# A hybrid attention and RWKV-7 layer on one core: transposing transfers sent piece by piece, and weight transfers issued three tiles ahead

## The chip, the core and the metric

The kernel runs on one core of a Trainium2 chip. Its engines run side by side and wait for each other through semaphores: TensorE (PE, matmuls and their weight loads PEld), VectorE (DVE), ScalarE (ACT), GpSimd (POOL) and SyncE (SP), which here does nothing but issue DMA transfers. Each engine takes its instructions in the order in which the built program holds them, SP its transfers too. The metric is the device time of one execution in microseconds (us), the median over runs.

## The reference

One layer over 256 tokens of width 4096. One projection of the input (4096 x 18640 columns) feeds 16 heads of forgetting attention ("fox"), 32 heads of RWKV-7 time mixing and a gate path; an output projection (4096 x 4096) and a LayerNorm with residual follow.

```python
proj = jnp.einsum('bsd,dc->bsc', x, w_in)
fox_out = _fox_attention(fq, fk, fv, log_sigmoid(ff + f_bias))   # causal softmax with decay, 16 heads of 128
rw = rw + (rw_prev - rw) * mu_shift                              # shift by one token, then r, k, v, decay, a
kk = kk / jnp.maximum(jnp.linalg.norm(kk, axis=-1, keepdims=True), 1e-12)
y = _rwkv7_scan(rh, decay, kh, vh, -kk, kk * ah)
# S_t = S_{t-1} diag(decay_t) + (S_{t-1} a_t) b_t^T + v_t k_t^T ;  y_t = S_t r_t, 32 heads of 64
y = groupnorm(y) * gn_gain + gn_bias + jnp.sum(rh * kh * r_k, axis=-1, keepdims=True) * vh
h = jnp.concatenate([fox_out, y], axis=-1) * jax.nn.silu(z)
x = layernorm(ALPHA * x + jnp.einsum('bsc,cd->bsd', h, w_out))
```

## The kernel before, in words

**The stream of weight tiles.** The input projection is cut into 8 groups n of 4 blocks b (two blocks of recurrent columns, b = 0 for r and k and b = 1 for the values, then b = 2 and 3, each with the queries, keys and gates of one pair of heads); the output projection into 8 blocks. A block has 16 weight tiles of 128 x 1024 float32 (512 KB), called `w<n>_<b>_<q>` or `wo<b>_<q>`. Every tile is loaded by SP (L217), rounded to fp32r on ACT (the high part `h`, L140) and subtracted on DVE (the low part `l`, L141, "the split"); then PE does 12 matmuls of 512 columns with it, four times the three products x_high·w_high, x_low·w_high, x_high·w_low (L146 to L148). Four loaded tiles, four high parts and three low parts have room. So the split of tile q can start only when PE has ended tile q-3, and a transfer can start only when the split four tiles earlier is done.

**Side work.** What the heads need is written as generators (`prepare`, `rwkv`, `fox`, `unload`). `slot()` advances each of them by one `yield` and is called twice per tile; the table `W` and constants such as `V_AT` count these slots. A scheduler that builds the program then orders each engine's instructions; only where the code says `keep_in_program_order` does an instruction stay where it was written. The resulting order repeats from group to group.

**The solve.** In `rwkv(n)` the recurrence is turned into triangular systems that DVE solves in 31 steps, each a multiply (L537, `prod`) and a reduction (L540, `xc`); every step reads the one before, and both grow wider from step to step. It needs the factors `Nb`, copied out from DRAM.

**Transposing through DRAM.** `turn` (L272 to L278) takes a tile that DVE has transposed in squares of 32 x 32, sends it to DRAM in four transfers (one per 32 partitions), and another transfer reads it back. So go the factors (`BKt<-BK`, L277, then L527), the values (`vt<-UV`, then `vv<-vt` at L549), the projections (`bt<-bk`, then `raw`, `fq`, `fk`, `zf`, `zr`) and the attention weights (`fpt<-lg`, then `pT` at L706). `gate` makes a gated head output `h` and stores it (`hd<-hl`, L366); the output projection reads it back. All these transfers stand in the one queue of SP, among the weight tiles.

```python
    def weights(name):
        while len(ready) < 3 and stream:
            fetch()                       # one transfer, and the split behind it
    ...
            if t == V_AT + 2:             # in step 8 of the solve
                vdr = turn(vst, f"vt{n}")
```

## Time and profile before

| | |
|---|---|
| three runs | 2053.64 us median (2051.88 to 2056.26) |
| profiled execution, its own time | 2051.41 us |
| its span (first to last instruction) | 2049.6 us |
| PE busy | 1963.8 us (96%), 10063 matmuls |
| PE's weight loads | 1592.2 us (78%) |
| DVE busy | 1396.4 us (68%) |
| ACT busy | 969.9 us (47%) |
| POOL busy | 84.6 us (4%) |
| DMA | 434.03 MB, mean 212 GB/s |
| granted PE clock, mean | 0.980 |

The span is the profiled execution alone; 1.8 us of its time lie outside. In the profile's rows tile names have lost their group and block, so `w_11l` is the low part of the twelfth tile of some block. In a timeline a row has the start in us, the length, engine, line, operation, output<-input and how often; brackets hold the idle time before it and what ended that. PE's matmuls are pipelined, so the distance between two starts, not the length, is what one costs. A row of windows has, per engine, busy us and the number of instructions, then the granted clock, the DMA share and GB/s.

### The profile page before, as it was taken

The page shows a single profiled execution, that of the slowest core. Times are in us where ns is not written, and L with a number is a line of the kernel's source. Part 1 is how long each engine was busy: PE and PEld are TensorE (multiplying, and loading weights), DVE is VectorE, ACT ScalarE, POOL GpSimd, SP SyncE. Part 2 cuts the span into 40 slices and gives each one's busy share as a digit, 9 for nine tenths or more (in the row PEclk, how much of TensorE's full clock was granted, in tenths as well). Part 3 has the DMA queues.
Part 4 walks back from the last instruction along what each step waited for, and adds up shares of the span by engine and source line. Part 5 has one row for each costly group of instructions (what it writes and reads, how often), then busy time and mean ns, then how long its engine had stood idle before and what let it go on. Part 6 is the DMA issues. An engine that isn't in the chain of part 4 may idle for free.

```text
span 2049.6 us, 28216 instructions
## 1 busy us (share of the span) xinstructions
PE 1963.8 (96%) x10063; PEld 1592.2 (78%) x10063; DVE 1396.4 (68%) x2242; ACT 969.9 (47%) x1455; POOL 84.6 (4%) x111
## 2 busy tenths in 40 slices
PE   9997999999989998999899999998999899999998
PEld 8885778777877787778777877787778778888886
DVE  6587568756775687568756876687558757755555
ACT  6543455345534553455345534553455355443333
POOL 0010001000100010001000100010001000000000
PEclk9998999999999999999999999999999999999999
DMA  9577667766786678667766776677667786866664
GB/s 334 153 206 212 184 202 223 224 189 204 215 230 187 202 221 229 186 200 227 222 189 198 224 217 200 193 219 211 206 187 217 227 306 221 254 197 198 200 185 174
DMA packets 328241, 434.03 MB, mean 212 GB/s; under 512 B 198370, under 2 KB 228852, under 8 KB 328100
## 3 DMA queue, kind: packets, MB, share of 16 engines
q1 hardware_dynamic: 327668, 431.81, 69.9%
q8 instruction: 79, 1.29, 0.3%
q14 instruction: 62, 0.51, 0.1%
q10 hardware_dynamic: 432, 0.43, 0.1%
HBM read 395.56 MB, written 36.59 MB: 211 GB/s over the span
## 4 chain that ended last, share of the span: by engine, by line
PE 79%; DVE 11%; DMA 5%; issue 2%; ACT 2%; SPq 1%; ACTq 0%; DVEq 0%
PE acc L146 19%; PE acc L148 18%; PE acc L147 18%; PE oacc L831 6%; PE oacc L833 6%; PE oacc L832 6%; DMA w<-in_w_main_dram 4%; DVE xc L540 3%; DVE prod L537 3%; SPq L277 1%; PE yp L649 1%; PE gp L492 1%; PE up L624 1%; PE rh L597 1%; DVE w_11l L141 1%
## 5 line engine op out<-in xcount | busy, mean ns | idle before, releaser
L148 PE MATMUL acc<-w_11l,x 128*128 128x512 f32 x124 | 54.1, 449 | 33.3 <-DVE w_11l L141 33.3
L141 DVE TENSOR_TENSOR w_5l<-w,w_5h 128x1024 fp32r<-128x1024 f32 x31 | 38.9, 1254 | 66.9 <-ACT w_5h L140 36.8
L540 DVE TENSOR_REDUCE xc<-prod 128x8 f32<-128x16 f32 (+30 forms) x248 | 73.3, 296 | 7.6
L537 DVE TENSOR_TENSOR prod<-Nb,xc 128x8 f32<-128x8 f32 (+30 forms) x248 | 72.2, 291 | 7.6
L141 DVE TENSOR_TENSOR w_6l<-w,w_6h 128x1024 fp32r<-128x1024 f32 x31 | 37.8, 1219 | 45.6 <-ACT w_6h L140 29.1
L146 PE MATMUL acc<-w_5h,x 128*128 128x512 f32 x124 | 54.0, 436 | 14.7 <-ACT w_5h L140 14.7
L141 DVE TENSOR_TENSOR w_4l<-w,w_4h 128x1024 fp32r<-128x1024 f32 x31 | 38.0, 1225 | 38.7 <-PE acc L148 32.6
L140 ACT CAST w_5h<-w 128x1024 fp32r<-128x1024 f32 x31 | 32.5, 1050 | 67.0 <-DMA w<-in_w_main_dram 42.6
L141 DVE TENSOR_TENSOR w_12l<-w,w_12h 128x1024 fp32r<-128x1024 f32 x31 | 37.9, 1222 | 37.3 <-ACT w_12h L140 35.6
L146 PE MATMUL acc<-w_4h,x 128*128 128x512 f32 x124 | 51.1, 412 | 11.1 <-ACT w_4h L140 11.1
L141 DVE TENSOR_TENSOR w_8l<-w,w_8h 128x1024 fp32r<-128x1024 f32 x31 | 37.9, 1223 | 33.1 <-PE acc L148 18.5
L140 ACT CAST w_15h<-w 128x1024 fp32r<-128x1024 f32 x31 | 32.6, 1052 | 57.6 <-PE acc L147 20.6
L148 PEld LDWEIGHTS acc<-w_11l,x 128*128 128x128 f32 x124 | 25.7, 214 | 41.7 <-DVE w_11l L141 36.7
L140 ACT CAST w_11h<-w 128x1024 fp32r<-128x1024 f32 x31 | 32.5, 1048 | 54.1 <-DMA w<-in_w_main_dram 44.6
L141 DVE TENSOR_TENSOR w_3l<-w,w_3h 128x1024 fp32r<-128x1024 f32 x31 | 37.9, 1223 | 27.2 <-PE acc L148 25.3
L148 PE MATMUL acc<-w_5l,x 128*128 128x512 f32 x124 | 52.7, 425 | 2.4 <-DVE w_5l L141 2.4
L146 PE MATMUL acc<-w_12h,x 128*128 128x512 f32 x124 | 50.8, 410 | 4.2 <-ACT w_12h L140 4.1
L146 PE MATMUL acc<-w_11h,x 128*128 128x512 f32 x124 | 51.7, 417 | 1.6 <-ACT w_11h L140 1.6
L140 ACT CAST w_8h<-w 128x1024 fp32r<-128x1024 f32 x31 | 32.6, 1051 | 43.0 <-PE acc L147 32.4
L140 ACT CAST w_12h<-w 128x1024 fp32r<-128x1024 f32 x31 | 32.6, 1050 | 41.8 <-DMA w<-in_w_main_dram 35.8
L141 DVE TENSOR_TENSOR w_9l<-w,w_9h 128x1024 fp32r<-128x1024 f32 x31 | 37.8, 1220 | 20.8 <-PE acc L148 10.8
L684 POOL TENSOR_SCALAR_AFFINE_SELECT nb<-nb 128x128 f32<-128x128 f32 x32 | 22.9, 716 | 701.0 <-DMA nb<-ncd 420.0
(811 smaller groups left out, 6575.8 us busy)
## 6 DMA issues: line engine op xcount, KB each, us to landing
w<-in_w_main_dram SPq DMA_DIRECT2D x496, 512.0 KB, 4.7
wo<-in_w_o_dram SPq DMA_DIRECT2D x128, 512.0 KB, 3.4
bt<-bk SPq DMA_DIRECT2D x88, 128.0 KB, 3.9
Nb<-nd SPq DMA_DIRECT2D x16, 512.0 KB, 4.9
wr<-in_w_main_dram SPq DMA_DIRECT2D x15, 512.0 KB, 6.1
hd<-hl SPq DMA_DIRECT2D x29, 256.0 KB, 2.6
h<-hd SPq DMA_DIRECT2D x29, 256.0 KB, 6.3
raw<-bt SPq DMA_DIRECT2D x16, 256.0 KB, 4.5
```

Source lines behind the costliest of these rows:

```text
L140: nc.scalar.copy(hi[:, :n], src[:, :n])
L141: nc.vector.tensor_tensor(lo[:, :n], src[:, :n], hi[:, :n].bitcast(F32), ALU.subtract)
L146: nc.tensor.matmul(acc[:, :n], xs[k][:, 0, tt], hi[:, o : o + n], start=(k == 0), stop=False)
L147: nc.tensor.matmul(acc[:, :n], xs[k][:, 1, tt], hi[:, o : o + n], start=False, stop=False)
L148: nc.tensor.matmul(acc[:, :n], xs[k][:, 0, tt], lo[:, o : o + n], start=False, stop=(k == KT - 1))
L277: nc.sync.dma_start(out=d[:, :, :, a, :].rearrange("q i m t -> i m q t"), in_=s[B * a : B * (a + 1)])
L537: first = nc.vector.tensor_tensor(prod[:, :, :, s + 1 :], nb[:, :, s : s + 1, s + 1 :].to_broadcast([P, 2, NJ, w]), xc[:, :, :, s + 1 :], ...
L540: nc.vector.tensor_reduce(xc[:, :, :, s : s + 1], prod[:, :, :, s:], AX.X, ALU.add)
L684: nc.gpsimd.affine_select(out=nb[:, m, :], in_=nb[:, m, :], compare_op=ALU.is_ge, fill=NEG, base=0, pattern=[[-1, P]], channel_multiplier=1)
L831: nc.tensor.matmul(acc, ht[k][:, 0, tt], hi, start=(k == 0), stop=False)
L832: nc.tensor.matmul(acc, ht[k][:, 1, tt], hi, start=False, stop=False)
L833: nc.tensor.matmul(acc, ht[k][:, 0, tt], lo, start=False, stop=(k == KT - 1))
```

## The change

- **Weights ahead.** `fetch` is split: `load` issues a transfer and keeps up to three loaded tiles in `raws`; `fetch` tops that up first and then splits the oldest. The numbers of buffers stay.
- **Pinned transfers.** A new helper `issue` sends side transfers under `keep_in_program_order`; `turn` is now a generator that yields after every two of its four transfers (or after each one, with `each=1`).
- **Inside the solve.** Factors and values are no longer sent ahead of the solve and at fixed steps of it, but by a generator `turns` that advances once per step: four factor transfers one at a time, two slots later their reading back, then the values' squares, their four transfers one at a time, their reading back and the product `bon`. `V_AT` is gone, and the wait before the solve is `W["d1"]` in one piece, as long as before in all.
- **Stores of h.** The store waits `SENT` = 3 slots behind its source; at most one earlier store may be waiting.
- **Preparation.** `prepare` yields at five more places and waits two slots behind its pinned reciprocal, and `W["np"]` goes from 6 to 4. The copies `UV<-SV` on ACT are pinned.

No computation, size or number of transfers changes. The diff, cut to its core ("..." where lines are left out):

```diff
-V_AT = 6
-W = {"fo": 3, "vs": 2, "np": 6, "gp": 5, "tp": 4, "d1": 8, "d2": 12, "xp": 3, "fs": 4, "fp": 5}
+W = {"fo": 3, "vs": 2, "np": 4, "gp": 5, "tp": 4, "d1": 8, "d2": 12, "xp": 3, "fs": 4, "fp": 5}
...
-    def fetch():
+    raws = []
+
+    def load():
         if stream:
             name, src = stream.pop()
             raw = wpool.tile([P, 1024], F32, tag="wr", name=name, bufs=4)
             nc.sync.dma_start(out=raw, in_=src.rearrange("p k c -> p (k c)"))
+            raws.append((name, raw))
+
+    def fetch():
+        while len(raws) < 3 and stream:
+            load()
+        if raws:
+            name, raw = raws.pop(0)
...
-    def turn(src, name):
+    def issue(out, src):
+        tc.keep_in_program_order(nc.sync.dma_start(out=out, in_=src))
+
+    def turn(src, name, each=2):
...
         for a in range(4):
-            nc.sync.dma_start(out=d[:, :, :, a, :].rearrange("q i m t -> i m q t"), in_=s[B * a : B * (a + 1)])
+            issue(d[:, :, :, a, :].rearrange("q i m t -> i m q t"), s[B * a : B * (a + 1)])
+            if a % each == each - 1:
+                yield
         return d
...
         if far:
-            nc.sync.dma_start(out=hd[k], in_=flat(hl).bitcast(F32))
+            storing.append(k)
+            yield from wait(SENT)
+            issue(hd[k], flat(hl).bitcast(F32))
             kept_h.add(k)
+            storing.remove(k)
...
-        nc.vector.reciprocal(n2, n2)
+        yield
+        tc.keep_in_program_order(nc.vector.reciprocal(n2, n2))
+        yield from wait(2)
...
-        yield from wait(2)
-        bd = turn(BK.rearrange("p u c t -> p (u c) t"), f"BKt{n}")
-        yield from wait(2)
+        yield from wait(W["d1"])
         BKt = rp.tile([P, 2, NCH, P], F32, tag="shl", name=f"BKt{n}")
-        nc.sync.dma_start(out=BKt.rearrange("p u c t -> p (u c t)"), in_=bd.rearrange("q i g a t -> (q i) (g a t)"))
-        yield from wait(W["d1"] - 4)
+
+        def turns():
+            d = yield from turn(BK.rearrange("p u c t -> p (u c) t"), f"BKt{n}", 1)
+            yield from wait(2)
+            issue(BKt.rearrange("p u c t -> p (u c t)"), d.rearrange("q i g a t -> (q i) (g a t)"))
+            yield
+            vst = UV[0].rearrange("p u c v -> p (u c v)").rearrange("p (m q) -> p m q", m=2)
+            for a in range(2):
+                tc.keep_in_program_order(nc.vector.transpose(vst[:, a, :], vs_[n][:, a, :]))
+            yield from wait(3)
+            d = yield from turn(vst, f"vt{n}", 1)
+            yield from wait(2)
+            vv[n] = rp.tile([P, 2, S], F32, tag="s2", name=f"vv{n}")
+            issue(vv[n], turned_back(d))
+            yield from wait(4)
+            nc.vector.tensor_tensor(flat(bon), flat(bon), flat(vv[n]), ALU.mult)
...
+        other = turns()
...
-            if t == V_AT:
...
+            next(other, None)
...
-            nc.scalar.copy(UV[j][o], SV[j][o])
+            tc.keep_in_program_order(nc.scalar.copy(UV[j][o], SV[j][o]))
```

How this moves the instructions, at three places of group 2. First SP, early in block 1 (`w2_1_q` are its weight tiles; `fpt3` and `pT3` the attention weights of head 3, `bt2_0` and `raw` the r and k columns, `hd` a store of h). Before:

```order
L217 DMA w2_1_4_4566<-in_w_main_dram 128x1024
L277 DMA fpt3_4509<-lg3_4450 96x4x32 x4
L277 DMA bt2_0_4561<-bk2_0_4514 64x16x32
L706 DMA pT3_4539<-fpt3_4509 128x384
L277 DMA bt2_0_4561<-bk2_0_4514 64x16x32 x3
L366 DMA hd_848<-hl6_4585 128x512
L217 DMA w2_1_5_4597<-in_w_main_dram 128x1024
L771 DMA raw4_4589<-bt2_0_4561 128x2x256
L217 DMA w2_1_6_4623<-in_w_main_dram 128x1024
```

Now:

```order
L218 DMA w2_1_6_4563<-in_w_main_dram 128x1024
L281 DMA fpt3_4550<-lg3_4453 96x4x32 x4
L281 DMA bt2_0_4575<-bk2_0_4501 64x16x32 x2
L281 DMA pT3_4584<-fpt3_4550 128x384
L281 DMA bt2_0_4575<-bk2_0_4501 64x16x32 x2
L218 DMA w2_1_7_4588<-in_w_main_dram 128x1024
L218 DMA w2_1_8_4608<-in_w_main_dram 128x1024
L281 DMA raw4_4606<-bt2_0_4575 128x2x256
L218 DMA w2_1_9_4636<-in_w_main_dram 128x1024
L218 DMA w2_1_10_4673<-in_w_main_dram 128x1024
```

The block of side transfers stood behind tile 4 and held tile 5 behind the store of h; now it stands behind tile 6, and the store has left it for a place behind `raw5`, five weight tiles further on.

Second, DVE in block 2, where the solve meets the splits (`prod` and `xc` are the steps, the last number how wide). Before:

```order
L540 TENSOR_REDUCE xc2_5158<-prod2_5157 128x8
L537 TENSOR_TENSOR prod2_5157<-Nb2_5017,xc2_5158 128x8x20
L141 TENSOR_TENSOR w2_2_11l_5168<-w2_2_11_5165,w2_2_11h_5167 128x1024
L540 TENSOR_REDUCE xc2_5158<-prod2_5157 128x8
L537 TENSOR_TENSOR prod2_5157<-Nb2_5017,xc2_5158 128x8x21
L141 TENSOR_TENSOR w2_2_12l_5190<-w2_2_12_5187,w2_2_12h_5189 128x1024
L540 TENSOR_REDUCE xc2_5158<-prod2_5157 128x8
```

Now:

```order
L141 TENSOR_TENSOR w2_2_11l_5157<-w2_2_11_5118,w2_2_11h_5156 128x1024
L141 TENSOR_TENSOR w2_2_12l_5175<-w2_2_12_5136,w2_2_12h_5174 128x1024
L579 TENSOR_TENSOR prod2_5191<-Nb2_5057,xc2_5192 128x8
L582 TENSOR_REDUCE xc2_5192<-prod2_5191 128x8
L579 TENSOR_TENSOR prod2_5191<-Nb2_5057,xc2_5192 128x8x2
L582 TENSOR_REDUCE xc2_5192<-prod2_5191 128x8
L579 TENSOR_TENSOR prod2_5191<-Nb2_5057,xc2_5192 128x8x3
L582 TENSOR_REDUCE xc2_5192<-prod2_5191 128x8
L579 TENSOR_TENSOR prod2_5191<-Nb2_5057,xc2_5192 128x8x4
L582 TENSOR_REDUCE xc2_5192<-prod2_5191 128x8
L579 TENSOR_TENSOR prod2_5191<-Nb2_5057,xc2_5192 128x8x5
L141 TENSOR_TENSOR w2_2_13l_5204<-w2_2_13_5154,w2_2_13h_5203 128x1024
```

Before, 19 steps and the multiply of the 20th stood between the splits of tiles 10 and 11. Now tile 11 and tile 12 are split before the solve begins, and steps and splits alternate from there; the last step stands right ahead of the split of tile 5 of block 3.

Third, SP from the factors to the values (`BKt2` factors, `vt2` and `vv2` values, `bt2_2` and `fq4` the columns of block 2). Before:

```order
L277 DMA BKt2_5096<-BK2_4636 256x4x32 x4
L217 DMA w2_2_11_5165<-in_w_main_dram 128x1024
L217 DMA w2_2_12_5187<-in_w_main_dram 128x1024
L527 DMA BKt2_5119<-BKt2_5096 128x1024
L217 DMA w2_2_13_5209<-in_w_main_dram 128x1024
L217 DMA w2_2_14_5233<-in_w_main_dram 128x1024
L277 DMA vt2_5255<-UV0_2_5038 64x8x32 x4
L217 DMA w2_2_15_5260<-in_w_main_dram 128x1024
L217 DMA w2_3_0_5284<-in_w_main_dram 128x1024
L549 DMA vv2_5282<-vt2_5255 128x2x256
```

Now, from the middle of that stretch on:

```order
L218 DMA w2_3_3_5295<-in_w_main_dram 128x1024
L281 DMA vt2_5317<-UV0_2_5078 64x8x32
L218 DMA w2_3_4_5324<-in_w_main_dram 128x1024
L281 DMA vt2_5317<-UV0_2_5078 64x8x32 x2
L218 DMA w2_3_5_5348<-in_w_main_dram 128x1024
L281 DMA vt2_5317<-UV0_2_5078 64x8x32
L218 DMA w2_3_6_5373<-in_w_main_dram 128x1024
L281 DMA bt2_2_5387<-bk2_2_5319 64x16x32 x2
L281 DMA vv2_5398<-vt2_5317 128x2x256
L281 DMA bt2_2_5387<-bk2_2_5319 64x16x32 x2
L218 DMA w2_3_7_5402<-in_w_main_dram 128x1024
L218 DMA w2_3_8_5430<-in_w_main_dram 128x1024
```

The four transfers of the factors, before in one piece ahead of tile 11, now stand at four places between `w2_2_14` and `w2_3_1`; the values' transfers are spread likewise, and their reading back `vv2` is now among the transfers of `bt2_2`, ahead of weight tiles 7 and 8 of block 3. On DVE the product that reads `vv2` has moved from behind the split of tile 15 to between the splits of tiles 6 and 7 of block 3.

44 lines of the change are left out of this document (21 added, 23 removed).

## The prediction

> **What bounds the kernel now.** I began with the page's busy times:
>
> ```profile
> PE 1963.8 (96%) x10063; PEld 1592.2 (78%) x10063; DVE 1396.4 (68%) x2242; ACT 969.9 (47%) x1455; POOL 84.6 (4%) x111
> ```
>
> PE is busy for 96% of the span, so what can be won is its idle time and any time at a lowered clock. PE's waits (who for whom, total us, how often, longest) name nearly all of it:
>
> ```profile
> PE acc L148 <- DVE w_11l L141: 33.3, 8, 4.8
> PE acc L146 <- ACT w_5h L140: 14.7, 6, 2.8
> PE acc L146 <- ACT w_4h L140: 11.1, 1, 11.1
> PE acc L146 <- ACT w_12h L140: 4.1, 6, 0.8
> PE acc L148 <- DVE w_15l L141: 3.1, 5, 0.8
> ...
> PE acc L146 <- ACT w_6h L140: 2.1, 1, 2.1
> ```
>
> The wait for `w_11l` comes in the solve, once in each of groups 1 to 7 (33.3 / 4.8 is seven); `w_5h` and, in group 1, `w_6h` in block 1 of the same groups; `w_4h` once, in group 0. What one costs including its aftermath is read from windows, by counting matmuls: a stretch without stalls, block 1 and the solve of group 2, and group 0:
>
> ```profile
> 1800.00:1850.00 50.00, 50.00 (x222) 41.42 (x221) 26.54 (x26) 20.20 (x20) 0.00 (x0) 1.00 0.65 197
> 502.66:512.66 10.00, 7.23 (x24) 5.25 (x23) 5.35 (x10) 5.29 (x8) 0.11 (x1) 0.83 0.96 315
> 573.00:583.00 10.00, 5.19 (x16) 3.89 (x15) 9.27 (x26) 2.94 (x4) 0.00 (x0) 0.69 0.70 210
> 176.00:206.00 30.00, 18.08 (x67) 13.65 (x66) 22.75 (x49) 10.35 (x15) 0.00 (x0) 0.77 0.67 192
> ```
>
> Undisturbed, 222 matmuls take 50 us: 0.225 us each, 2.70 us for a tile of 12. The other windows lose what is left beyond their matmuls: block 1 10 - 24 x 0.225 = 4.6 us, the solve 10 - 16 x 0.225 = 6.4, group 0 30 - 67 x 0.225 = 14.9. That is more than the waits, because PE runs slowly behind them (start of each matmul in block 1 of group 2):
>
> ```profile
> 503.32 0.39 PE L148 MATMUL acc<-w_4l,x 128*128 128x512 f32 x1
> 503.54 0.39 PE L146 MATMUL acc<-w_4h,x 128*128 128x512 f32 x1
> ...
> 507.31 0.50 PE L146 MATMUL acc<-w_5h,x 128*128 128x512 f32 x1 [2.25 <-ACT w_5h L140]
> ...
> 508.57 0.79 PE L148 MATMUL acc<-w_5l,x 128*128 128x512 f32 x1 [0.53 <-DVE w_5l L141]
> 509.16 0.63 PE L146 MATMUL acc<-w_5h,x 128*128 128x512 f32 x1
> 509.59 0.63 PE L147 MATMUL acc<-w_5h,x 128*128 128x512 f32 x1
> ```
>
> 0.22 us from start to start before, 0.43 after; the window has a granted clock of 0.83. The wait (2.25, and 0.53 for the low part) makes 2.8 of the 4.6, so a tail of 1.8 follows it. All together: 7 x 4.6 = 32, 7 x 6.4 = 45, 14.9, and the short waits for `w_12h` and `w_15l`, 4.1 + 3.1: 99 us. The rest (start and end of the program) the change leaves alone.
>
> Next I asked why each tile is late. Block 1, SP's timeline, then DVE's, then ACT's:
>
> ```profile
> 488.48 2.57 SPq L277 DMA_DIRECT2D fpt<-lg  x4
> ...
> 494.22 2.34 SPq L277 DMA_DIRECT2D bt<-bk  x3
> 501.38 0.33 SPq L366 DMA_DIRECT2D hd<-hl  x1
> 501.76 0.43 SPq L217 DMA_DIRECT2D w<-in_w_main_dram  x1
> ```
>
> ```profile
> 490.82 1.23 DVE L141 TENSOR_TENSOR w_2l<-w,w_2h 128x1024 fp32r<-128x1024 f32 x1
> ...
> 500.93 0.42 DVE L364 TENSOR_TENSOR hl<-h,hl 128x256 fp32r<-128x256 f32 x1 [0.47 <-ACT hl L363]
> ```
>
> ```profile
> 506.22 1.04 ACT L140 CAST w_5h<-w 128x1024 fp32r<-128x1024 f32 x1 [5.32 <-DMA w<-in_w_main_dram]
> ```
>
> From 496.56 (494.22 + 2.34) SP stands before the store `hd`, until DVE has made `hl` (501.35). Tile 5 is behind it in the queue, is issued at 501.76 and cast at 506.22: 4.5 us from issue to cast. In the solve the cause is another. ACT's cast of tile 11, and DVE's timeline:
>
> ```profile
> 571.25 1.05 ACT L140 CAST w_11h<-w 128x1024 fp32r<-128x1024 f32 x1 [6.58 <-DMA w<-in_w_main_dram]
> ```
>
> ```profile
> 566.88 0.17 DVE L537 TENSOR_TENSOR prod<-Nb,xc 128x8 f32<-128x8 f32 x1
> ...
> 578.25 1.22 DVE L141 TENSOR_TENSOR w_11l<-w,w_11h 128x1024 fp32r<-128x1024 f32 x1
> 579.39 0.33 DVE L540 TENSOR_REDUCE xc<-prod 128x8 f32<-128x168 f32 x1
> ...
> 581.50 0.34 DVE L537 TENSOR_TENSOR prod<-Nb,xc 128x176 f32<-128x176 f32 x1
> ...
> 591.39 0.42 DVE L540 TENSOR_REDUCE xc<-prod 128x8 f32<-128x256 f32 x1
> 591.73 1.22 DVE L141 TENSOR_TENSOR w_15l<-w,w_15h 128x1024 fp32r<-128x1024 f32 x1
> 592.86 0.68 DVE L551 TENSOR_TENSOR bon<-bon,vv 128x512 f32<-128x512 f32 x1
> ...
> 594.99 0.71 DVE L760 STREAM_TRANSPOSE bk<-bk 128x512 f32<-128x512 f32 x1 [0.31 <-ACT bk L869]
> ```
>
> The high part was ready at 572.30, but DVE splits tile 11 only at 578.25: since 566.88 it works through solve steps that stand ahead of the split in its order. In group 0 it is ACT whose order holds the tile, behind a copy that waits for DVE's last steps:
>
> ```profile
> 189.49 0.61 ACT L575 COPY UV<-SV 64x512 f32<-64x512 f32 x1 [7.77 <-DVE SV L572]
> ...
> 191.04 1.04 ACT L140 CAST w_4h<-w 128x1024 fp32r<-128x1024 f32 x1
> ```
>
> **The change part by part.**
>
> Weights ahead, and the store behind. In block 1 SP now meets tile 6, then the block of side transfers, then tile 7. Tile 6 needs the buffer that the split of tile 2 frees (490.82 + 1.23 = 492.05). The block takes 8.1 us (488.48 to 496.56), so tile 7 is issued by 500.2, reaches its cast at 504.7 and is ready at 505.7. PE ended tile 4 at 505.1 (507.31 - 2.25) and without a stall starts tile 7 two tiles later, at 510.5: 4.8 us to spare, or 2.1 if the attention weights themselves come a tile later. The store, now behind `raw5`, waits where only later tiles are behind it, and three slots after its source it has nothing left to wait for. So 32 us go; if that cover were gone, 4.6 us come back per group.
>
> The solve. DVE's work is the same, the order new: the splits of tiles 11 and 12 first, then steps and splits in turn, the last step ahead of the split of tile 5 of block 3. The work between: the steps 566.88 to 578.25 = 11.4 (with two squares of the values), 579.39 to 591.73 = 12.3 less three splits of 1.14 (578.25 to 579.39) = 8.9, together 20.3; two squares of `bk` at 0.71 = 1.4; nine splits = 10.3. Sum 32.0. PE's time for it: tile 12 can be split when PE ends tile 9, so the solve starts 1.2 us into tile 10, and the third matmul of tile 5 of block 3 needs the low part 0.45 us into a tile that is eleven on: 11 x 2.70 + 0.45 - 1.2 = 28.9. DVE is 3.1 us late, and something is late before that: up to the split of tile 1 of block 3 stand 22 multiplies and 21 reductions (566.88 to 581.84, less two splits, 12.7), the squares of `bk` (1.4) and five splits (5.7), 19.8, against 7 x 2.70 + 0.45 - 1.2 = 18.1. PE waits 1.7 us at tile 1, a tail of 1.8 follows as in block 1, and in these 3.5 us DVE catches up with its 3.1. So 3.5 us per group in place of 6.4, 24.5 in seven groups. Ends: nothing, if PE has enough else to do there, and 6.4, if the late tile only has another number. I take 3.5, as its durations are DVE's own rows.
>
> The Trainium skill, page "TensorE: Matmul & The Clock Gate", section "Why this matters for your kernels", asks for no idle gap over about 3 us, after which the clock falls to half. By that rule a wait of 1.7 us has no tail, the price is DVE's 3.1, and the sum comes out 2.8 us lower, 1990; the rows above show half speed behind a wait of 2.25 us, so I keep the tail.
>
> Group 0. In the new order its casts no longer stand behind the copies, but nine of the last steps (up to 0.42 by the row at 591.39, and as much for the multiply) stand between the splits of tiles 6 and 7, about 7.4 us against the 1.56 that a tile leaves beside its split, and the softmax of head 0 stands ahead of tile 9. Between 3.5 and 14.9 I take 11.
>
> The short waits (7.2 us). Tiles 12 and 15 come through in time, but other tiles now stand behind the same transfers. Between 0 and 7.2 I take 3.
>
> Preparation spread, `np`, the pinned copies: no instruction more. The chain of each pair moves two tiles later, hidden under the weight stream that fills the next block; in the last group under the 28 tiles of the output projection that need nothing of it. Were it bare, it would cost two tiles once, 5.4 us.
>
> Sum: 99 before; 0 + 24.5 + 11 + 3 = 38.5 after. The profiled execution's own time of 2051.4 becomes 1990.9; the median of the runs was 2.2 higher, so 1993.
>
> **The rivals.**
>
> The solve only moves its stall (2013): block 1 is cured, the solve still costs 6.4, 7 x 2.9 more. For it: DVE has 32.0 us of work in 28.9, whatever the order. Against: the stall is met in smaller pieces.
>
> The solve is hidden wholly (1968): 24.5 less. For it: three low parts are ready at the start; against: the same sum.
>
> The queue gains nothing, because buffers and not positions hold the transfers (2025): the 32 us of block 1 stay. For it: the same bubble in every group. Against: the buffer for tile 6 is free at 492.05, 9 us before tile 5 was sent. The Trainium skill, page "Perfetto Trace Analysis", section "Optimization Strategy", reads such consistent bubbles as a possible lack of room for the next tile; that would be this rival. That the change does not do what it says would give the same time.
>
> Slower (2063): `bon`. Values before, SP's timeline and the median time from issue to landing:
>
> ```profile
> 570.76 4.30 SPq L277 DMA_DIRECT2D vt<-UV  x4
> ...
> 581.76 0.38 SPq L549 DMA_DIRECT2D vv<-vt  x1
> ```
>
> ```profile
> vt<-UV SPq DMA_DIRECT2D x32, 64.0 KB, 5.3
> vv<-vt SPq DMA_DIRECT2D x8, 256.0 KB, 4.4
> ```
>
> ```profile
> 593.58 0.91 ACT L553 ACTIVATE bon<-bon,prm 128x256 f32<-128x256 f32 x2 [6.41 <-DVE bon L551]
> ```
>
> `vv` was sent 11 us ahead of the product on DVE (592.86), which did not wait. Now the product stands between the splits of tiles 6 and 7 of block 3, and the last piece of the values is sent behind tile 5, whose buffer the split of tile 1 frees. From there 1.1 us for the piece (4.30 / 4), 5.3 to land, 4.4 for `vv`: 10.8 us, about the four tiles that DVE takes to get there. If `vv` lands late, DVE stands with all splits behind it, and ACT's casts behind its own use of `bon` (which even before waited 6.41). With about 2 us of slack in ready tiles, `vv` 12 us late costs 10 per group, 7 x 10 = 70. It decides from 8.7 + 2 us on. Against: nothing that long stands between the piece and `vv`.
>
> **How the numbers follow.** Forecast 0.56, stall moved 0.20, hidden 0.10, buffers 0.08, slower 0.06. The bounds alone give 1993 - 24.5 - 3 = 1966 below; above, 7 x 2.9 for the solve, 4 for the short waits and 4 for group 0 give 2021, and the buffers' case 2025; so 1966 to 2026, with only the slower case and mixtures outside. Less than 0.2%, 4 us, is what a measurement of this kernel cannot tell from no change. Faster 0.92, same 0.02, slower 0.06.
>
> **What would show it.** No PE wait for `w_5h` or `w_6h` in block 1, and `w_11l` gone from PE's waits (right for queue and order); a wait of 1 to 3 us for the low part of tile 1 of block 3 in groups 1 to 7, with DVE busy without a gap from tile 10 on (right for the solve; a wait with idle DVE would make the sum wrong); a wait near 5 us in group 0 for tile 7 or 9. Wrong would be DVE idle ahead of `bon` for several us, or PE waiting for `pT`, `T` or `BKt`.

## The result and the profile after

| | before | changed | |
|---|---|---|---|
| median of 4 runs each | 2052.76 us (2048.71 to 2056.26) | 1993.01 us (1984.19 to 1995.43) | ratio 0.9702 (95%: 0.9667 to 0.9737) |
| profiled execution, its own time | 2051.41 us | 1992.19 us | -59.2 |
| its span | 2049.6 us | 1990.4 us | -59.2 |
| granted PE clock, mean | 0.980 | 0.990 | |

The total came out at the forecast of 1993, but not as its sum had it. The busy times of the changed kernel, and PE's waits with the total, how often, and the longest:

```profile
PE 1948.0 (98%) x10063; PEld 1583.7 (80%) x10063; DVE 1384.1 (70%) x2242; ACT 962.3 (48%) x1455; POOL 79.6 (4%) x111
```

```profile
PE acc L146 <- ACT w_7h L140: 10.6, 7, 2.3
PE acc L148 <- DVE w_7l L141: 7.9, 8, 4.2
PE acc L148 <- DVE w_1l L141: 7.7, 8, 1.5
...
PE acc L146 <- ACT w_9h L140: 1.6, 1, 1.6
PE acc L146 <- ACT w_15h L140: 1.5, 1, 1.5
```

The waits for `w_11l`, `w_5h`, `w_6h` and `w_12h` are gone. In their place stands one for the high part of tile 7, seven times, and one for the low part of tile 1. The windows say where: a quiet stretch, block 1 and the solve of group 2, group 0.

```profile
1800.00:1850.00 50.00, 50.00 (x222) 41.40 (x221) 29.60 (x31) 19.54 (x20) 0.00 (x0) 1.00 0.62 187
494.00:510.00 16.00, 14.10 (x56) 10.85 (x55) 11.44 (x19) 10.42 (x16) 0.11 (x1) 0.89 0.81 273
573.00:593.00 20.00, 18.82 (x82) 14.75 (x81) 17.80 (x36) 7.96 (x11) 0.00 (x0) 1.00 0.83 213
176.00:206.00 30.00, 23.16 (x89) 17.70 (x88) 23.27 (x51) 8.29 (x15) 0.00 (x0) 0.89 0.57 166
```

Block 1 loses 16 us less 52 tile matmuls at 0.225 and 0.6 us for four small side ones (`fop`), 3.7 us, at a clock of 0.89; the solve 20 - 82 x 0.225 = 1.5 us at full clock; group 0 30 - 89 x 0.225 = 10.0 us.

In block 1 the wait is no longer for a transfer. ACT's timeline, PE's and SP's in group 2:

```profile
487.19 1.05 ACT L140 CAST w_6h<-w 128x1024 fp32r<-128x1024 f32 x1 [1.56 <-DMA w<-in_w_main_dram]
496.74 0.37 ACT L747 COPY fo<-fop 128x256 f32<-128x256 f32 x1 [8.50 <-PE fop L745]
497.61 0.40 ACT L379 CAST hl<-h 128x256 fp32r<-128x256 f32 x1 [0.49 <-DVE h L376]
497.92 1.04 ACT L140 CAST w_7h<-w 128x1024 fp32r<-128x1024 f32 x1
```

```profile
495.89 0.59 PE L744 MATMUL fop<-pT,vt 128*128 128x256 f32 x2
...
499.01 0.50 PE L146 MATMUL acc<-w_7h,x 128*128 128x512 f32 x1 [1.38 <-ACT w_7h L140]
...
500.27 0.54 PE L148 MATMUL acc<-w_7l,x 128*128 128x512 f32 x1 [0.53 <-DVE w_7l L141]
...
501.03 0.63 PE L147 MATMUL acc<-w_7h,x 128*128 128x512 f32 x1
501.46 0.63 PE L148 MATMUL acc<-w_7l,x 128*128 128x512 f32 x1
```

```profile
490.32 1.77 SPq L218 DMA_DIRECT2D w<-in_w_main_dram  x2
```

Tile 7 was issued at 490.32, but ACT stood for 8.50 us before `fo`, the copy of an attention head's product out of PSUM. That product, `fop`, is reached by PE only at 495.89, inside tile 6. Behind `fo` in ACT's order come the cast of `hl`, which waits for DVE, and then the cast of tile 7, at 497.92. PE waits 1.38 us for the high part and 0.53 for the low part, and then starts matmuls 0.43 us apart for a while.

In the solve, DVE's timeline and PE's:

```profile
557.47 1.22 DVE L141 TENSOR_TENSOR w_12l<-w,w_12h 128x1024 fp32r<-128x1024 f32 x1 [1.49 <-PE acc L148]
558.61 0.17 DVE L579 TENSOR_TENSOR prod<-Nb,xc 128x8 f32<-128x8 f32 x1
...
576.55 1.22 DVE L141 TENSOR_TENSOR w_1l<-w,w_1h 128x1024 fp32r<-128x1024 f32 x1
...
588.54 1.22 DVE L141 TENSOR_TENSOR w_5l<-w,w_5h 128x1024 fp32r<-128x1024 f32 x1
589.67 1.22 DVE L141 TENSOR_TENSOR w_6l<-w,w_6h 128x1024 fp32r<-128x1024 f32 x1
590.80 0.69 DVE L565 TENSOR_TENSOR bon<-bon,vv 128x512 f32<-128x512 f32 x1
```

```profile
577.83 0.50 PE L148 MATMUL acc<-w_1l,x 128*128 128x512 f32 x1 [0.96 <-DVE w_1l L141]
...
589.81 0.73 PE L148 MATMUL acc<-w_5l,x 128*128 128x512 f32 x2 [0.21 <-DVE w_5l L141]
```

From the first step (558.61) to the end of the split of tile 1 (576.55 + 1.22) pass 19.2 us; PE waits 0.96 us there and 0.21 at tile 5, and no slow stretch follows. The product `bon` starts as soon as the split of tile 6 lets it, so the values had landed.

In group 0 ACT's cast of tile 9 stands behind the softmax of head 0, and DVE's split of tile 7 behind the last steps of the solve:

```profile
181.76 1.22 DVE L141 TENSOR_TENSOR w_6l<-w,w_6h 128x1024 fp32r<-128x1024 f32 x1
...
190.34 1.22 DVE L141 TENSOR_TENSOR w_7l<-w,w_7h 128x1024 fp32r<-128x1024 f32 x1
```

```profile
199.61 0.40 ACT L724 ACTIVATE lg<-lg,fst 128x128 f32<-128x128 f32 x1 [6.13 <-DVE fst L723]
...
200.50 1.03 ACT L140 CAST w_9h<-w 128x1024 fp32r<-128x1024 f32 x1
```

### The profile page after: what moved, and what is told of

It is laid out like the page before. It is cut to its first block, busy times and chain, and to the rows that moved or that the text cites. A ratio compares the mean times of both kernels' runs of the same rounds, so it can differ in the third digit from the quotient of the medians.

```text
span 1990.4 us, 28153 instructions
## 1 busy us (share of the span) xinstructions
PE 1948.0 (98%) x10063; PEld 1583.7 (80%) x10063; DVE 1384.1 (70%) x2242; ACT 962.3 (48%) x1455; POOL 79.6 (4%) x111
## 4 chain that ended last, share of the span: by engine, by line
PE 85%; DVE 11%; issue 2%; ACT 1%; DMA 1%; ACTq 0%; DVEq 0%; SPq 0%
PE acc L146 20%; PE acc L148 20%; PE acc L147 19%; PE oacc L860 6%; PE oacc L861 6%; PE oacc L862 6%; DVE prod L579 3%; DVE xc L582 3%; PE yp L678 1%; PE gp L517 1%; DMA w<-in_w_main_dram 1%; PE up L653 1%; PE rh L626 1%; DVE w_7l L141 1%; DVE w_15l L141 0%
## 5 line engine op out<-in xcount | busy, mean ns | idle before, releaser
L141 DVE TENSOR_TENSOR w_0l<-w,w_0h 128x1024 fp32r<-128x1024 f32 x31 | 37.8, 1220 | 53.0 <-ACT w_0h L140 46.9
L146 PE MATMUL acc<-w_7h,x 128*128 128x512 f32 x124 | 55.8, 450 | 10.6 <-ACT w_7h L140 10.6
L141 DVE TENSOR_TENSOR w_6l<-w,w_6h 128x1024 fp32r<-128x1024 f32 x31 | 37.9, 1222 | 35.9 <-ACT w_6h L140 19.3
L148 PE MATMUL acc<-w_7l,x 128*128 128x512 f32 x124 | 54.4, 439 | 7.9 <-DVE w_7l L141 7.9
L148 PE MATMUL acc<-w_1l,x 128*128 128x512 f32 x124 | 49.1, 397 | 7.7 <-DVE w_1l L141 7.7
L141 DVE TENSOR_TENSOR w_7l<-w,w_7h 128x1024 fp32r<-128x1024 f32 x31 | 37.9, 1224 | 26.8 <-ACT w_7h L140 16.4
L140 ACT CAST w_5h<-w 128x1024 fp32r<-128x1024 f32 x31 | 32.6, 1051 | 46.3 <-PE acc L147 24.5
L147 PE MATMUL acc<-w_7h,x 128*128 128x512 f32 x124 | 53.8, 434 | 0.0
L141 DVE TENSOR_TENSOR w_10l<-w,w_10h 128x1024 fp32r<-128x1024 f32 x31 | 37.9, 1223 | 22.0 <-PE acc L148 18.2
L141 DVE TENSOR_TENSOR w_5l<-w,w_5h 128x1024 fp32r<-128x1024 f32 x31 | 37.9, 1222 | 22.0 <-PE acc L148 13.5
L141 DVE TENSOR_TENSOR w_11l<-w,w_11h 128x1024 fp32r<-128x1024 f32 x31 | 37.9, 1221 | 19.4 <-PE acc L148 12.0
L146 PE MATMUL acc<-w_15h,x 128*128 128x512 f32 x124 | 49.8, 401 | 1.5 <-ACT w_15h L140 1.5
L146 PE MATMUL acc<-w_8h,x 128*128 128x512 f32 x124 | 50.3, 406 | 0.8 <-ACT w_8h L140 0.8
L146 PE MATMUL acc<-w_9h,x 128*128 128x512 f32 x124 | 49.0, 395 | 1.6 <-ACT w_9h L140 1.6
L146 PE MATMUL acc<-w_5h,x 128*128 128x512 f32 x124 | 50.6, 408 | 0.0
```

The lines of the kernel that those rows point to most:

```text
L140: nc.scalar.copy(hi[:, :n], src[:, :n])
L141: nc.vector.tensor_tensor(lo[:, :n], src[:, :n], hi[:, :n].bitcast(F32), ALU.subtract)
L146: nc.tensor.matmul(acc[:, :n], xs[k][:, 0, tt], hi[:, o : o + n], start=(k == 0), stop=False)
L147: nc.tensor.matmul(acc[:, :n], xs[k][:, 1, tt], hi[:, o : o + n], start=False, stop=False)
L148: nc.tensor.matmul(acc[:, :n], xs[k][:, 0, tt], lo[:, o : o + n], start=False, stop=(k == KT - 1))
```

## The experiments

Each is one profiled execution unless said otherwise; the kernel before took 2052.6 to 2054.2 us beside them. Four executions of the changed kernel spread over 11 us (1984.19 to 1995.43), so a difference of that size between two single times says little by itself; the readings below go by the waits in the traces. A slow stretch is a run of matmuls that start 0.43 us apart in place of 0.2265. The table sums, for each trace, what the tile matmuls started later than the steady 0.2265 us, where that was over 0.15 us: waits and slow stretches together. Pricing the side matmuls between them otherwise moves a cell by up to 4 us. The last column also has block 0 of these groups, the first 100 us and the output projection.

| kernel | time, us | group 0 | block 1, groups 1-7 | blocks 2 and 3, groups 1-7 | all |
|---|---|---|---|---|---|
| before | 2051.4 | 17.5 | 32.8 | 62.0 | 122.2 |
| changed | 1992.2 | 10.4 | 27.0 | 15.2 | 61.9 |
| e1 `fo` later | 1969.4 | 12.0 | 1.1 | 18.7 | 40.5 |
| e2 no lead | 2007.9 | 13.3 | 9.6 | 44.1 | 76.4 |
| e3 solve sent whole | 2011.4 | 7.1 | 18.0 | 50.6 | 84.7 |
| e4 steps in order | 1961.6 | 2.6 | 1.2 | 14.8 | 35.3 |
| e6 solve alone | 2032.8 | 12.1 | 31.6 | 46.9 | 99.1 |
| e7 store unpinned | 2003.7 | 9.4 | 37.9 | 18.7 | 73.5 |
| e8 steps in order, earlier | 1951.7 | 2.1 | 5.2 | 5.0 | 19.8 |
| e9 lead alone | 2015.7 | 15.3 | 6.4 | 55.9 | 86.2 |
| e10 preparation whole | 1999.4 | 3.0 | 34.6 | 19.9 | 65.8 |
| e12 head's weights sent whole | 1970.1 | 11.4 | 3.2 | 16.9 | 40.1 |

**What holds tile 7 in block 1?** First the copy `fo` alone was moved (e1):

```diff
-        nc.scalar.copy(o, op[:, :S])
+        if i % 2:
+            yield from wait(2)
+            tc.keep_in_program_order(nc.scalar.copy(o, op[:, :S]))
+        else:
+            nc.scalar.copy(o, op[:, :S])
```

> The changed kernel with one edit: in every second head of the attention (the one whose output product falls into block 1) the copy `fo` out of PSUM is traced two slots later and pinned there, so that on ACT the cast of tile 7 stands ahead of `fo` and of the cast of `hl`, not behind them; on DVE the split of tile 7 stands ahead of `h`. No instruction more or less. Theory A (ACT's order holds tile 7: the profile after shows ACT idle for 8.50 us before `fo`, which needs a product that PE reaches only inside tile 6, while tile 7 was issued 490.32 and, with the 4.5 us from issue to cast of the profile before, could be cast at 494.8, be ready at 495.9 and split at 497.0; PE ends tile 6 at 497.5): the wait for `w_7h` in block 1 goes from 10.6 us in seven places to under 2, its slow tail with it, and the time falls by 27 us, to 1965 (1963 to 1970). Theory B (the transfer of tile 7 is what comes late, sent behind the block of side transfers): ACT waits for the transfer instead, PE's wait stays near 1.5 us at each place, and the time stays within 4 us of 1992.

1969.4 us, at the upper end of theory A. The timelines of ACT (two rows), DVE and PE of this kernel:

```profile
490.81 1.05 ACT L140 CAST w_7h<-w 128x1024 fp32r<-128x1024 f32 x1 [7.41 <-DMA w<-in_w_main_dram]
493.19 0.37 ACT L749 COPY fo<-fop 128x256 f32<-128x256 f32 x1 [1.33 <-PE fop L745]
```

```profile
491.89 1.22 DVE L141 TENSOR_TENSOR w_7l<-w,w_7h 128x1024 fp32r<-128x1024 f32 x1 [5.32 <-ACT w_7h L140]
```

```profile
493.92 0.40 PE L146 MATMUL acc<-w_7h,x 128*128 128x512 f32 x1
```

Now the cast waits for the transfer, ends at 491.86, and PE goes from tile 6 to tile 7 without a gap. Block 1 falls from 27.0 to 1.1 us. So ACT's order was the cause; the transfer itself has 1.3 us to spare (the split ends at 493.1, PE needs it two matmuls into the tile, at 494.4).

What put `fop` so late? In e12 the four pieces of the attention weights go out in one slot again, and ACT's order is left as it is:

```diff
-            ld = yield from turn(lg, f"fpt{i}")
+            ld = yield from turn(lg, f"fpt{i}", 8)
```

> The changed kernel with one edit: the four pieces of the attention weights `fpt` are sent in one slot, not two a slot over two slots. The product `fop` of the odd heads then stands behind the sixth matmul of tile 5 of block 1, not behind the eighth of tile 6, 14 matmuls or 3.2 us earlier on PE; on ACT `fo` and `hl` keep their places ahead of the cast of tile 7, and the solve keeps its order. So far PE's first wait for tile 7 followed the place of `fop`: behind the second matmul of tile 6 0.17 us (the changed kernel without its lead), behind the eighth 1.54, behind the twelfth 2.52 (group 1, and the kernel with the preparation whole). Theory A (ACT's cast of tile 7 waits for that product, and the two slots are what put it late): no wait for `w_7h` from group 2 on, at most 0.5 us, and 1992 - 25 = 1967 (1964 to 1973), as with the copy moved behind the cast. Theory B (the place of `hl` and of its store, which now comes ahead of tile 9 in SP's order, holds tile 9 in its place): a wait of 1 to 2 us for tile 9 a group, 1975 to 1985. Theory C (the place of `fop` does not matter): 1992.

1970.1 us, theory A: block 1 loses 3.2. The same wait goes away when the product comes 14 matmuls earlier as when the copy steps aside. With the places of `fop` in e2 and e10 the wait follows matmul by matmul: behind the second of tile 6 0.17 us, the eighth 1.54, the twelfth 2.52 (starts beyond 0.2265 us).

Then the lead alone, put into the kernel before (e9: `load`, `raws` and the new `fetch`, nothing else):

> The kernel before with one part of the change: the weights' transfers up to three tiles ahead of their splits; stores, sends, solve and preparation as before. In SP's order of block 1 tile 5 now stands ahead of three of the four pieces of `bt` and tile 6 ahead of the store `hd`; on ACT the copy `fo` and the cast of `hl` still stand ahead of the cast of tile 6. On DVE the 41 instructions between the splits of tiles 10 and 11 stay. Theory A (in block 1 places hold the tile, so the lead cures the wait for `w_5h`, and ACT's order gives a smaller one at tile 6, 0 to 2.3 us; the solve keeps its 7.1 less the wait for `w_15l`): 7 x 2.3 to 4.6 us less in block 1, 5 in the solve: 2053 - 21 to 37 = 2016 to 2032. Theory B (buffers hold the transfers, one of the prediction's rivals): block 1 keeps its 4.6 and the time is 2045 to 2057.

2015.7 us, at the lower end of theory A. A window over block 1 of group 2, and one over the solve:

```profile
488.00:505.00 17.00, 16.87 (x75) 13.64 (x75) 10.14 (x16) 8.48 (x13) 0.11 (x1) 1.00 0.81 238
560.00:575.00 15.00, 10.19 (x35) 7.88 (x34) 14.04 (x37) 5.28 (x6) 0.00 (x0) 0.77 0.70 207
```

17 us with 75 matmuls: nothing is lost in block 1, while the solve loses 15 - 35 x 0.225 = 7.1. So buffers do not hold the transfers, places do, and the lead by itself is worth 38 us in the kernel before. Here `fop` still stands inside tile 3, and ACT is past `fo` in time.

The opposite, the changed kernel without its lead (e2: the old `fetch`):

> The changed kernel with the weights' transfers traced as before: each tile's transfer together with its split, not up to three tiles ahead of it. In SP's order of block 1 the tiles keep their places (tile 6, the side transfers, tile 7); in DVE's order of the solve the steps stand in larger clumps: 15 of them ahead of the split of tile 14 and 12 ahead of that of tile 15, 9 ahead of tile 3 of block 3. Theory A (the places in the engines' orders decide): block 1 stays as it is, 3.8 us a group; the solve, by its rows laid against PE's 2.70 us a tile, waits 1.2, 2.0 and 1.6 us for the low parts of tiles 14, 15 of block 2 and 3 of block 3 where the changed kernel waits 1.1 for tile 1, some 3.5 us more in each of seven groups: 1992 + 25 = 2017 (2008 to 2025). Theory B (the prediction's: the lead itself gives the transfers their time): waits of ACT's casts for the transfers come back in block 1, PE's wait for `w_5h` or `w_6h` there, 4.6 us a group beside the solve's, and the time goes to 2025 or above. If neither counts, 1992.

2007.9 us, 0.1 below theory A's range, and by parts that differ from it. PE's waits:

```profile
PE acc L148 <- DVE w_3l L141: 12.5, 7, 2.0
PE acc L148 <- DVE w_15l L141: 12.4, 7, 1.8
PE acc L148 <- DVE w_14l L141: 6.9, 7, 1.6
```

The three waits of the solve came where and about as long as laid out (1.8, 1.8 and 1.0 us each). But block 1 fell to 9.6, where `fop` happens to come six matmuls earlier. In the changed kernel the lead thus pays through DVE's order, in the solve.

The stores (e7), not pinned and not three slots later:

```diff
-            storing.append(k)
-            yield from wait(SENT)
-            issue(hd[k], flat(hl).bitcast(F32))
+            nc.sync.dma_start(out=hd[k], in_=flat(hl).bitcast(F32))
             kept_h.add(k)
-            storing.remove(k)
```

> The changed kernel with the stores of `hl` issued as before: at once behind the cast that makes them, not pinned, and not three slots later. In SP's order of block 1 the store now stands between the first `raw` and tile 9, where SP waits for `hl` (made at 498.5 in the profile after) with tiles 9 to 11 behind it; in the changed kernel tile 9 was issued at 493.44 already. Tile 9 would then be issued at 498.9, cast at 503.4, ready at 504.5; with the wait for tile 7 as it is PE reaches tile 9 at 506.9. Theory A: nothing is lost in block 1, and the time stays within 4 us of 1992. Theory B (the prediction's: the store's place was what held block 1): 2 to 4.6 us a group come back, 2006 to 2024.

2003.7 us, between the two theories, and by neither's mechanism. SP's timeline and ACT's, group 7:

```profile
1478.55 0.33 SPq L218 DMA_DIRECT2D w<-in_w_main_dram  x1
1482.61 0.33 SPq L382 DMA_DIRECT2D hd<-hl  x1
1482.98 0.58 SPq L281 DMA_DIRECT2D bt<-bk  x1
```

```profile
1494.75 0.37 ACT L744 COPY fo<-fop 128x256 f32<-128x256 f32 x1 [9.79 <-PE fop L742]
...
1497.78 1.04 ACT L140 CAST w_7h<-w 128x1024 fp32r<-128x1024 f32 x1 [1.76 <-DMA w<-in_w_main_dram]
```

Not the store that I had named gets in the way but the one before it: from 1478.88 to 1482.61 SP stands before a store that now leads the block of side transfers. The block is late, `fop` with it, and ACT's wait before `fo` grows to 9.79 us; in this group tile 7's transfer then comes late as well (1.76). In groups 2 to 7 `fop` stands behind the twelfth matmul of tile 6 in place of the eighth, and PE's waits for the high part of tile 7 sum to 18.3 us in place of 10.6; block 1 loses 10.9 us more.

**What decides the solve?** First with the old sending of factors and values (e3: the two removed parts of the diff back in place of `turns`):

> The changed kernel with the solve as it was before: factors sent in one piece ahead of it, the values' squares and transfers inside it by step numbers, nothing in it pinned but its first step; the rest of the change stays. On DVE 41 solve instructions (39 of them steps) now stand between the splits of tiles 12 and 13. Theory A (what counts is how many steps stand ahead of a split): PE waits 5.1 us at tile 13 in each of groups 1 to 7, with a slow tail of 1.5 to 2.2 us as before the change, some 6.8 us a group in place of the 1.5 now: 1992 + 7 x 5.3 = 2029 (2022 to 2034). Theory B (the sum of DVE's work decides, as the prediction had it, and the sending of pieces adds nothing): waits sum to about 2 us a group, and the time stays within 8 us of 1992.

2011.4 us. PE's waits:

```profile
PE acc L149 <- DVE w_13l L142: 33.5, 7, 5.0
PE acc L147 <- ACT w_7h L141: 10.6, 7, 2.3
```

Theory A holds for the solve: 33.5 us in seven places, 5.0 at most, at tile 13, and 50.6 us in blocks 2 and 3. The time misses A's range mostly because block 1 lost only 18.0 us with the very same waits (10.6), as in six of seven groups no slow stretch followed them; group 0 lost 3.3 us less as well. This is the prediction's first rival, a stall that only moves its place, and with the rest of the change in place the sending in pieces is what prevents it.

The same part alone in the kernel before (e6):

> The kernel before with one part of the change: factors and values sent piece by piece inside the solve, squares of the values there too; no lead, stores and preparation as before. On DVE 9, 7, 15 and 12 steps now stand between the splits of tiles 10 to 13, in place of 14 and 25 between 10 and 11. Theory A (the clump ahead of each split decides): by the rows laid against 2.70 us a tile PE waits 2.0 us at tile 12, 2.0 at tile 13 and 1.6 at tile 1 of block 3, together 5.6 us a group with or without a tail, in place of 7.1 with its tail; block 1 keeps its 4.6: 2053 - 7 x 1.5 = 2042 (2036 to 2053). Theory B (sending singly is what cured the solve): the solve falls to the 1.5 us a group of the changed kernel, 2053 - 7 x 5.6 = 2014.

2032.8 us, 3 below A's range and far from B: blocks 2 and 3 keep 46.9 us of 62.0. Sent in pieces, but without the lead, the solve still has clumps of 15 and 12 steps. The waits stand at the tiles that were laid out, but those for tiles 12 and 13 are about 1.1 and 1.3 us on average, not 2.0 (tile 1: 1.6).

Then every step pinned in its place (e4, on top of e1):

```diff
-            if not t:
-                tc.keep_in_program_order(first)
+            tc.keep_in_program_order(first)
```

> The first kernel of this set (`fo` later) with one more edit: each of the 31 steps of the solve is pinned in the order of the program, not the first alone. On DVE 4 instructions of the solve then stand between any two splits (6 once), and the last step moves from ahead of tile 5 of block 3 to behind tile 10 of it. Theory A (the clumps make the wait; the sum of 32.0 against 28.9 us that the prediction used held only because the order put the last step ahead of tile 5): the waits for `w_1l` and `w_5l` of block 3 vanish in seven groups (10 us) and the one for `w_7l` in group 0 shrinks (5 to 10 us): 12 to 20 us under the first kernel of this set, near 1950. Theory B (DVE's work is too much for the stretch, whatever the order): the same 1 to 2 us a group are lost at a later tile, and the time is within 4 us of the first kernel's. Theory C (the chain behind the solve, T and the products that need it, becomes late): PE waits for T in each group, and the time rises above the first kernel's.

1961.6 us, 7.8 under e1 and less than A said. The waits for tiles 1 and 5 are gone and group 0 falls to 2.6 us, but six times 2.0 us are lost at tile 13. DVE's timeline:

```profile
588.73 0.35 DVE L725 TENSOR_SCALAR lg<-lg,fst 128x256 f32<-128x256 f32 x1
...
594.74 1.22 DVE L141 TENSOR_TENSOR w_13l<-w,w_13h 128x1024 fp32r<-128x1024 f32 x1
```

Between the splits of tiles 12 and 13 stand 6.0 us of late steps, softmax and the values' means. Starting the solve three slots earlier (e8: `"d1": 5`) moves the steps ahead of them:

> The fourth kernel (copy `fo` later, every step of the solve pinned) with the solve begun three slots, 1.5 tiles, earlier (`d1` 5 in place of 8), where DVE stood idle for 1.49 us ahead of each of the splits of tiles 11 and 12. On DVE the steps then end ahead of tile 12 of block 3, and the softmax and the values' means no longer stand among the last of them. Theory A (the 2.0 us at tile 13 of block 3 come from 6.0 us of such work between the splits of tiles 12 and 13): the wait at tile 13 goes, six times 2.0 us: 1961.6 - 12 = 1949 (1945 to 1953). Theory B (the solve's own data, the square blocks behind `nd`, land too late for an earlier start, or the work is too much for the stretch): the first multiply waits for them or another tile takes the wait over, and the time stays within 4 us of 1961.

1951.7 us, theory A. Between the first 100 us and the end no gap over 1.7 us is left, and no slow stretch.

**The preparation** (e10: `prepare` of the kernel before, `np` 6):

> The changed kernel with the preparation of a pair as before: not spread by slots, `np` 6, its reciprocal not pinned. The solve then begins one to two tiles earlier; on ACT `fo` keeps its place ahead of the cast of tile 7 in block 1. Theory A (the prediction's: spreading costs and brings nothing by itself): within 4 us of 1992. Theory B (by DVE's rows against 2.70 us a tile the steps now stand otherwise: waits of 1.1, 0.2 and 1.1 us in the solve, 2.4 us a group in place of the 1.5): 1998 (1995 to 2002). Theory C (without the spreading DVE's work of the preparation stands in a piece ahead of a split in block 1 or 2): a new wait there of over 1 us a group, 2000 or more.

1999.4 us, theory B's time, by another sum: `fop` moved behind the twelfth matmul of tile 6, so block 1 lost 34.6 (27.0 changed), blocks 2 and 3 19.9 (15.2), and group 0 only 3.0 (10.4). Spreading did move things, by the orders that it changes elsewhere; the 7.2 us of time lie within the spread of the changed kernel.

**How long must a wait be for a slow stretch?** (e5)

```diff
+        for _ in range(LATER.get(name, 0)):
+            tc.keep_in_program_order(nc.vector.tensor_tensor(scr, scr, scr, ALU.mult))
```

> The changed kernel with delays of known size where nothing else disturbs PE: in blocks 2 to 6 of the output projection DVE does 14 to 23 extra multiplies of a scratch tile (128x256; 0.35 us each from start to start, by the row of 0.42 us) ahead of the split of tiles 4 and 10, ten places in all. A split is made up to 4.65 us before PE needs it, so the waits at these places are about 0.2, 0.6, 0.9, 1.3, 1.6, 2.0, 2.3, 2.7, 3.0 and 3.4 us. What is measured is the loss behind each wait, in matmuls that start 0.43 us apart in place of 0.225. Theory A (the prediction's: a wait of 1.7 us has a tail of 1.8 us): tails from the fifth or sixth place on, 1.4 to 2.2 us each. Theory B (the rule of the Trainium skill, page TensorE: Matmul & The Clock Gate, section Why this matters for your kernels, that only gaps over about 3 us lower the clock): a tail at the last place or two alone. Theory C (the wait's length alone does not decide; what lies in a stretch of several us around it counts): single waits up to 2 us have none, those over 2.5 all have one, and between them it differs from place to place. The time: 1992 plus the waits (18) plus 2 to 11 of tails, 2012 to 2021.

2039.3 us: the waits came out longer than meant, 31.2 us in all, since 19 extra multiplies took 8.70 us, 0.46 each and not 0.35:

```profile
1839.59 8.70 DVE L145 TENSOR_TENSOR scr<-scr 128x256 f32<-128x256 f32 x19
```

Two of the ten places on PE:

```profile
1780.27 0.73 PE L869 MATMUL oacc<-wo_4l,h 128*128 128x512 f32 x2 [2.63 <-DVE wo_4l L146]
1780.84 0.39 PE L867 MATMUL oacc<-wo_4h,h 128*128 128x512 f32 x1
1781.07 0.40 PE L868 MATMUL oacc<-wo_4h,h 128*128 128x512 f32 x1
```

```profile
1849.48 0.73 PE L869 MATMUL oacc<-wo_10l,h 128*128 128x512 f32 x2 [2.06 <-DVE wo_10l L146]
...
1850.42 0.63 PE L868 MATMUL oacc<-wo_10h,h 128*128 128x512 f32 x1
1850.85 0.63 PE L869 MATMUL oacc<-wo_10l,h 128*128 128x512 f32 x1
```

Behind 2.63 us of waiting the next starts are 0.23 us apart, behind 2.06 us 0.43. Of the ten places the two of 1.2 and 1.3 us and the one of 2.8 had no slow stretch, those of 2.2, 3.1 and over 3.8 had one (gaps from start to start, beyond 0.2265). So theory C: between about 2 and 3 us length alone does not decide. What does is in the last section.

**Both waits taken away**, five rounds of e8's kernel:

> The eighth kernel again, timed in rounds: the changed kernel with `fo` two slots later in every second head, every step of the solve pinned, the solve begun three slots earlier. Its one look gave 1951.65 us. If both waits of the changed kernel are gone in every execution: 1946 to 1956, a ratio to the kernel before of 0.948 to 0.953, against 0.9702 of the changed kernel. If the waits come and go with the chip's state: a spread of over 10 us and an upper end near 1965.

1953.15 us median (1952.75 to 1953.42), a ratio of 0.9512 to the kernel before (95%: 0.9494 to 0.9530), where the change alone has 0.9702. With both waits gone, the five executions lie within 0.7 us.

## Why the total was right and the sum was not

**The result hit, by errors that cancelled.** By the table the losses without the first 100 us and the output projection (7.5 and 7.2) were 114.7 us before and 54.7 after; the prediction had 99 and 38.5. Both are 16 short, so the difference, 60.0, was met by 60.5. That is luck: on the side after, block 1 has 27.0 us that were put at nothing, and blocks 2 and 3 have 15.2 where the solve alone was given 24.5.

**Block 1: the step that failed.** "So 32 us go": 27.0 stayed. The term was worked out along SP's queue and DVE's splits, and took the cast to start when the tile has landed. Tile 7 was indeed issued ahead of need, though 1.0 us before PE ended tile 4 and not 4.9, so with some 4 us less to spare than the 4.8 given; in e1 1.3 us are left, nearer to the second figure, 2.1. What the prediction left without a price is ACT's order. The attention's own product `fop` moved from behind tile 2 into tile 6; behind it stand `fo`, `hl` and then the cast. ACT's timeline before the change already had such a wait, there ahead of `hl`, which the store needs:

```profile
499.63 0.37 ACT L718 COPY fo<-fop 128x256 f32<-128x256 f32 x1 [5.26 <-PE fop L716]
```

The signs named for block 1 (no wait for `w_5h` or `w_6h`) both came true; none of them looked at tile 7. Moving the copy (e1) or the product (e12) brings about the 25 us that the prediction had already counted.

**The solve: right mechanism, mis-sized term.** The wait for the low part of tile 1 with DVE gapless was forecast and found. 24.5 us were given, the windows have 7 x 1.5 = 10.5. The wait was 1.0 us, not 1.7, as the work up to that split took 19.2 us and not 19.8; the tail of 1.8 us did not come in any of seven places; and from there to the split of tile 5 DVE needed 12.0 us, of which PE felt 0.2 in group 2. That DVE's 32.0 us must fit into 28.9 was no law: the end at tile 5 was set by the order, and with steps in order and an earlier start (e8) nothing waits.

**The tail.** The Trainium skill, page "TensorE: Matmul & The Clock Gate", section "Why this matters for your kernels", would have had no tail for 1.7 us; in the solve, with waits of 1.0 to 1.5, there was none. In block 1 that rule fails: 1.38 and 0.53 us of waiting were followed by a slow stretch in every group from 2 on (the last section).

**Group 0** was given 11 and has 10.0 in the window, at the two places named, 4.2 us for tile 7 and 1.6 for tile 9. **The short waits** were given 3; `w_15h` and its low part in the last group are 2.0. **What the 99 left out**: blocks 2 and 3 before lost 62.0 by the table against 45 + 7.2. About half of these 10 us lie around tiles 11 and 12 of block 2: some 7.1 us a group, where the window of group 2 gave 6.4.

**Preparation, priced at nothing**: undone, it costs 7.2 us in one execution, within the spread, and e10 shows no work of its own in that, only other places of `fop` and the steps. The pinned copies were not tried alone.

**The rivals.** "The solve only moves its stall" is what happens without the sending in pieces (e3), but not in the change. "Buffers hold it" fell with e9; there the consistent bubble that the Trainium skill, page "Perfetto Trace Analysis", section "Optimization Strategy", reads as a possible lack of room was a place in a queue. "Slower by `bon`" did not occur. Lead (38 us in the kernel before) and solve (21) add up to 59, like the whole change, but not by the same parts: alone, the lead wins block 1 and little of the solve; in the change, the two together win most of the solve, and the attention weights, sent over two slots, give most of block 1 back on ACT (e12).

## What to carry to other kernels

Follow a tile through every in-order queue on its way, the cast's engine too: ask what stands ahead of it there, and on which engine's work that waits. Where a fixed order mixes long side work with a stream of splits, lay the rows between two splits against the time of one tile; that gave the places of the solve's waits in e2, e3 and e6, and their sizes within 0.3 us in e2 and e3 (two of e6's came out 0.7 to 0.9 us shorter), where the sum over the stretch was wrong by a factor of two. Before taking a total as proof, compare the terms: this one was right with its largest wrong.

## What the runs showed of the hardware

**Between about 1.8 and 3.5 us a wait's length does not decide whether a slow stretch follows.** Over all fourteen traces (waits of PE between the first 20 and the last 30 us, pieces of over 0.5 us that lie under 1 us apart added up; a slow stretch here is four or more starts 0.40 to 0.47 us apart in the next 5 us):

| wait, us | under 1.5 | 1.5 to 2.0 | 2.0 to 2.5 | 2.5 to 4 | over 4 |
|---|---|---|---|---|---|
| with a slow stretch | 0 of 138 | 9 of 33 | 20 of 46 | 25 of 32 | 37 of 37 |

The shortest wait with one was 1.77 us, the longest without about 3.5. The same two waits of block 1 (2.24 us together) had it in six of six groups from 2 on in the changed kernel, in four of six in e5, in none of six in e3. The stretch takes 7 or 8 matmuls, about 3.3 us, and costs 1.4 to 1.8 us.

The Trainium skill, page "TensorE: Matmul & The Clock Gate", section "Part 1: The HAM clock gate (the "warmup" mystery)", has activity judged in a window of 3.4 us that runs freely. The traces agree, and show what decides.

In each of the eleven traces with three or more slow stretches, the times at which these end fit multiples of one period, 3.4133 or 3.4134 us by the fit, with under 0.03 us left over (13 of 13 in the kernel before, 8 of 8 in the changed one, 88 of 91 in all). Cut at these times, a trace falls into windows, and what counts is PE's idle time inside one window. With less than 1.95 us none of 5849 windows was followed by a slow one, with 1.95 to 2.15 us 18 of 24 were, with more all of 69. Cut half a period later, the same traces do not separate so: 31 of 5811 windows with less were followed by a slow one, and 18 of 71 with more were not. (Idle time is what a matmul started later than 0.2265 us, where that was over 0.1 us, slow ones aside; windows behind a slow one, or ahead of one with over 2 us of idle time, are left out.)

So a wait of 2.24 us brings a slow window where it falls into one window, and none where a border splits it: in group 2 of the changed kernel 2.46 us, with the small gaps beside it, lay in one window, in e3 1.54. The groups of the changed kernel follow each other in 197.9 to 198.0 us (once 198.5), where 58 periods are 197.97, so its six of six is one accident of phase met six times. For the solve's waits the most in one window of group 2 is 1.24 us, hence no tail there. The gap of about 3 us that the Trainium skill, page "TensorE: Matmul & The Clock Gate", section "Why this matters for your kernels", allows is too long: some 2 us in one window do it. Why the limit lies there no run shows.

**DVE instructions in a row cost more in e5 than I had taken from the rows.** Two products of the changed kernel on separate tiles start 0.33 us apart:

```profile
502.06 0.42 DVE L482 TENSOR_TENSOR lt<-s,eL 128x256 f32<-128x256 f32 x1
502.39 0.42 DVE L468 TENSOR_TENSOR k<-s,am 128x256 f32<-128x256 f32 x1
```

Those of e5 take 0.46 each; there each reads and writes one scratch tile. Whether this is the reason wasn't tried.
